# Row maxima of an 8192 x 8192 matrix: another order of the rows over the DMA engines, and one store per block

## The chip, the cores and the metric

The kernel runs on one core of a Trainium2 chip. The metric is the device time of one launch in microseconds: the median of three runs was 626.82 us (626.64 to 627.1). One more execution was taken with the hardware profiler; all readings of the trace are from that one.

## The reference

The input is a matrix of 8192 rows and 8192 columns in float32 (32 KB a row, 268.4 MB in all). The output has, for each row, the largest absolute value in it:

```python
def reference(x):
    return np.linalg.norm(x, ord=np.inf, axis=1)
```

## The kernel before

Each of the 128 partitions of the on-chip memory gets 64 of the rows. A tile `t` holds two rows of each partition (`B` = 2, `W` = 16384 columns, 64 KB a partition, 8.39 MB in all), and three such buffers rotate (`BUFS` = 3). All loads are issued by SyncE (SP) on one DMA queue, in the order of the program. Each waits until the buffer it writes is free, and in the tail for the semaphore that it takes over from an earlier DMA: eight completion semaphores go round over all the DMAs.

**Bulk.** 24 tiles (6 x `G`, `G` = 4) are loaded whole, one DMA each, L303. VectorE reduces each in one instruction (`absmax`, L296) to two columns of `r_bulk` (128 x 48). In memory a partition has eight rows in succession (256 KB) in each of the six blocks, and a tile takes two of them:

```python
x_b = x[:split].rearrange("(a p n b) c -> a n p (b c)", p=P, a=A, n=G, b=B)
```

**Tail.** The last 16 rows of each partition are 16 rows in succession (512 KB a partition). The first seven tail tiles are loaded in two to five pieces whose widths are listed in `TAIL` (L315), and every piece is reduced by itself to a column of `part`. The eighth is loaded in twelve pieces (`LAST`, L341), from 2176 columns down to 768. One instruction brings `part` together into 14 columns of `r_tail`; the last two columns of `r_tail` come from the last two pieces, each reduced together with the partial maxima of its row.

**Stores.** After the reduction of the tenth of the twelve pieces, ScalarE (ACT) stores `r_bulk` (L357). After the last reduction, SP stores `r_tail` (L359). These are all the DMAs there are besides the loads.

Functions run on the finished program (`start_first_load_early`, `drop_implied_waits`, `clear_partials_early`, `finish_on_pool`, `open_without_vector`): they put the first load ahead of the opening, drop waits that others imply, and let GpSimd end the program when the last store has landed. Neither these nor the reductions are touched by the change.

[...]

Of the kernel before, what the change touches and what calls it, by code (L numbers as in the profile page):

```python
# [12 lines left out]
F32 = mybir.dt.float32  # L13
# [4 lines left out]
TAIL = [  # L18
    [12672, 3712],
    [4992, 11392],  # L20
    [7040, 9344],
    [9344, 7040],
    [3584, 6784, 6016],
    [3968, 4224, 4736, 3456],
    [4096, 3584, 3200, 2944, 2560],
]
# [7 lines left out]


HEAD, STEP = 32, 8


def segments(loads, cols):

    out, at = [], 0
    for i, w in enumerate(loads):
        end = at + w
        while at < end:
            r = at // cols
            to = min(end, (r + 1) * cols)
            out.append((i, r, at - r * cols, to - at))
            at = to
    return out
# [201 lines left out]
@with_exitstack  # L251
def kernel(
    ctx: ExitStack,
    tc: tile.TileContext,
    x: bass.AP,
    out: bass.AP,
    G: int = 4,
    B: int = 2,
    BUFS: int = 3,
    PAD: int = 256,  # L260
    LINE: int = 128,
):
    nc = tc.nc
    P = nc.NUM_PARTITIONS
    rows, cols = x.shape
    W = B * cols


    n_tail = B * (len(TAIL) + 1)
    n_bulk_rows = rows // P - n_tail  # L270
    assert n_bulk_rows % (G * B) == 0
    A = n_bulk_rows // (G * B)
    split = n_bulk_rows * P
    x_b = x[:split].rearrange("(a p n b) c -> a n p (b c)", p=P, a=A, n=G, b=B)
    out_b = out[:split].rearrange("(a p n b) -> p a (n b)", p=P, a=A, n=G, b=B)
    x_t = x[split:].rearrange("(p t b) c -> t p (b c)", p=P, b=B)
    out_t = out[split:].rearrange("(p t) -> p t", p=P)

    outp = ctx.enter_context(tc.tile_pool(name="outp", bufs=1))
    sbuf = ctx.enter_context(tc.tile_pool(name="sbuf", bufs=BUFS))  # L280

    segs = [segments(loads, cols) for loads in TAIL]
    k_max = max(sum(r == b for _, r, _, _ in s) for s in segs for b in range(B))
    parts_of = [sum(r == b for r, _ in LAST) - 1 for b in range(B)]
    assert sum(parts_of) <= PAD

    r_bulk = outp.tile([P, A, G * B], F32)
    r_tail = outp.tile([P, n_tail], F32)
    part = outp.tile([P, n_tail - B, k_max], F32)
    used = [HEAD, A * G * B, n_tail, (n_tail - B) * k_max]  # L290
    gap = -sum(-(-n // STEP) * STEP for n in used) % LINE
    outp.tile([P, gap], F32, name="gap")
    nc.gpsimd.memset(part[:], 0.0)  # L293

    def absmax(o, i):
        return nc.vector.reduce_max(  # L296
            out=o, in_=i, axis=X, apply_absolute_value=True
        )

    for a in range(A):  # L300
        for n in range(G):
            t = sbuf.tile([P, W + PAD], F32, tag="t")
            nc.sync.dma_start(out=t[:, :W], in_=x_b[a, n])  # L303
            absmax(
                r_bulk[:, a, n * B : (n + 1) * B],
                t[:, :W].rearrange("p (b c) -> p b c", b=B),
            )

    for i, loads in enumerate(TAIL):
        t = sbuf.tile([P, W + PAD], F32, tag="t")  # L310
        todo = segs[i]
        seen = [0] * B
        at = 0
        for j, w in enumerate(loads):
            nc.sync.dma_start(out=t[:, at : at + w], in_=x_t[i][:, at : at + w])  # L315
            at += w
            for _, b, c, n in [s for s in todo if s[0] == j]:
                k, lo = seen[b], b * cols + c
                absmax(part[:, i * B + b, k : k + 1], t[:, lo : lo + n])
                seen[b] += 1  # L320

    def after(ins, first, kind):
        info = mybir.DependencyInfo(kind, mybir.DependencyReason.SCHED_ONLY)
        tc.add_manual_dep(ins.ins, first.ins.name, info, reason="order")


    t = sbuf.tile([P, W + PAD], F32, tag="t")
    left = parts_of[:]
    col = [0] * B
    at, slot = 0, {}  # L330
    ends = [w for _, w in LAST[-B:]]
    lo = W - sum(ends)
    for b in range(B):
        slot[b] = -(-lo // LINE) * LINE + ends[b]
        lo = slot[b] + parts_of[b]
    assert lo <= W + PAD
    for j, (b, w) in enumerate(LAST):
        final = left[b] == 0
        to = slot[b] - w if final else at
        frm = b * cols + col[b]  # L340
        nc.sync.dma_start(out=t[:, to : to + w], in_=x_t[len(TAIL)][:, frm : frm + w])  # L341
        col[b] += w
        if final:
            r = n_tail - B + b
            absmax(r_tail[:, r : r + 1], t[:, to : slot[b] + parts_of[b]])
        else:
            left[b] -= 1
            k = slot[b] + left[b]
            done = absmax(t[:, k : k + 1], t[:, to : to + w])
            at += w  # L350
        if j == 0:

            ins = absmax(r_tail[:, : n_tail - B], part[:])
            after(ins, done, mybir.DependencyClass.NoSync)
        if j == len(LAST) - 3:

            ins = nc.scalar.dma_start(out=out_b, in_=r_bulk[:])  # L357
            after(ins, done, mybir.DependencyClass.Sync)
    nc.sync.dma_start(out=out_t, in_=r_tail[:])  # L359
    nc.at_finalize(clear_partials_early)  # L360
    nc.at_finalize(drop_implied_waits)
    nc.at_finalize(start_first_load_early)
    nc.at_finalize(finish_on_pool)
    nc.at_finalize(open_without_vector)
# [30 lines left out]
```

## Time and profile before

| what | value |
|---|---|
| median of three runs | 626.82 us |
| the profiled execution, whole | 626.52 us |
| its span, first to last instruction | 623.9 us |
| VectorE busy | 552.4 us, 63 instructions |
| load queue (q1), share of 16 DMA engines' span | 99.7% |
| bytes read | 268.44 MB, 430 GB/s over the span |
| 24 bulk reductions | 413.3 us, 17.22 us each |

The profiler gives the start and duration of every instruction and every DMA packet, and for each wait what ended it. "SPq" and "ACTq" are the issuing sides of SP and ACT: an issue takes about 0.3 to 0.4 us there and the transfer goes on by itself. A packet record has a queue, a size, a start and a duration, but not the number of its DMA engine. In the chain of work, each step leads back from the last instruction to what released it. Groups are given by line, engine, operation and tiles, written as out<-in.

### The profile page before, as it was taken

To read this page: it belongs to the slowest core of one execution; us is meant where nothing else is said; L and a number is where in the kernel's file an instruction comes from. 1 tells how busy PE (TensorE), PEld (TensorE's weight loads), DVE (VectorE), ACT (ScalarE), POOL (GpSimd) and SP (SyncE) were. 2 spreads that over 40 slices of the span, in tenths; PEclk is the share of its full clock that TensorE was granted. 3 is DMA by queue.
4 is the path that set the end of the run, shared out by engine and by line. 5 is a ranking of instruction groups with operands and counts; after the bars stand their busy time and mean duration, and the time that the engine had idled before them with its cause. 6 is when DMAs were issued, how large, how long until landed. Compare 5 with 4: busy or idle time off the path is not lost.

```text
span 623.9 us, 151 instructions
## 1 busy us (share of the span) xinstructions
DVE 552.4 (89%) x63; POOL 0.3 (0%) x5
## 2 busy tenths in 40 slices
DVE  0588988889988899888898888988889999999999
POOL 0000000000000000000000000000000000000000
DMA  9999999999999999999999999999999999999998
GB/s 403 462 412 454 420 433 441 403 471 403 471 403 454 420 454 420 441 433 403 471 403 471 403 466 408 454 420 450 424 434 406 435 445 422 431 441 428 423 427 349
DMA packets 8849, 268.47 MB, mean 430 GB/s; under 512 B 1680, under 2 KB 1680, under 8 KB 3088
## 3 DMA queue, kind: packets, MB, share of 16 engines
q1 hardware_dynamic: 8064, 268.44, 99.7%
q10 hardware_dynamic: 784, 0.02, 0.1%
q14 instruction: 1, 0.01, 0.0%
HBM read 268.44 MB, written 0.03 MB: 430 GB/s over the span
## 4 chain that ended last, share of the span: by engine, by line
DMA 63%; DVE 36%; another core or an unknown queue 0%; DVEq 0%; issue 0%
DMA t<-in_x_dram 63%; DVE r_bulk L296 25%; DVE part L296 8%; DVE t L296 3%; DVEq L390 0%; DVE r_tail L296 0%
## 5 line engine op out<-in xcount | busy, mean ns | idle before, releaser
L296 DVE TENSOR_REDUCE r_bulk<-t 128x2 f32<-128x16384 f32 x24 | 413.3, 17220 | 70.5 <-DMA t<-in_x_dram 70.5
L296 DVE TENSOR_REDUCE part<-t 128x1 f32<-128x8192 f32 (+19 forms) x26 | 121.3, 4738 | 0.3
L296 DVE TENSOR_REDUCE t<-t 128x1 f32<-128x1792 f32 (+7 forms) x10 | 16.3, 1689 | 0.0
L296 DVE TENSOR_REDUCE r_tail<-t 128x1 f32<-128x772 f32 (+1 forms) x2 | 1.8, 947 | 0.0
L296 DVE TENSOR_REDUCE r_tail<-part 128x14 f32<-128x42 f32 x1 | 0.2, 185 | 0.0
L293 POOL MEMSET part<- 128x42 f32 x1 | 0.1, 133 | 0.0
L379 POOL MEMSET const-bfloat16-1.0<- 128x1 bf16 x1 | 0.1, 102 | 0.0
L379 POOL MEMSET const-uint8-127<- 128x1 uint8 x1 | 0.1, 102 | 0.0
L379 POOL MEMSET const-float32-0.0<- 128x1 f32 x1 | 0.1, 99 | 0.2 <-issue 0.2
L379 POOL MEMSET const-float32-1.0<- 128x1 f32 x1 | 0.1, 99 | 0.0
## 6 DMA issues: line engine op xcount, KB each, us to landing
t<-in_x_dram SPq DMA_DIRECT2D x2, 4672.0 KB, 37.5
t<-in_x_dram SPq DMA_DIRECT2D x2, 3520.0 KB, 36.2
t<-in_x_dram SPq DMA_DIRECT2D x1, 6336.0 KB, 36.4
t<-in_x_dram SPq DMA_DIRECT2D x1, 5696.0 KB, 40.5
t<-in_x_dram SPq DMA_DIRECT2D x2, 1792.0 KB, 34.3
t<-in_x_dram SPq DMA_DIRECT2D x1, 3392.0 KB, 37.6
t<-in_x_dram SPq DMA_DIRECT2D x1, 3008.0 KB, 44.2
t<-in_x_dram SPq DMA_DIRECT2D x1, 2496.0 KB, 27.3
```

The source lines that it names most:

```text
L293: nc.gpsimd.memset(part[:], 0.0)
L296: return nc.vector.reduce_max(out=o, in_=i, axis=X, apply_absolute_value=True)
L379: nc = _bacc.Bacc("TRN2", target_bir_lowering=False, num_devices=1)
```

## The change

The rows are dealt out otherwise. The 32 tiles, bulk and tail alike, are taken from four blocks of 11, 13, 5 and 3 tiles (`BLOCKS`). Within a block of n tiles, E is n x 64 KB, the n pairs of rows that one partition reads in succession. Partition 8e + i reads its rows at (16 i + e) x E from the block's start: e, from 0 to 15, is the outer dimension of the source of a load, i, from 0 to 7, the next. By the words of the change, e is the DMA engine and i the row of that engine. The first two blocks (24 tiles) are the bulk, the other two (8 tiles) the tail.

As a partition's rows of a block lie together, each block has its own store: `r_bulk` goes out in two stores and the first ten columns of `r_tail` in a third, all issued by ACT behind the same reduction as the one store before; the last six columns of `r_tail` go out from SP at the end, as all 16 did before. The sizes of all tiles, loads and reductions stay, and the order of the loads too. `r_bulk` loses a dimension without a change of size.

```diff
+LANES = 16
+BLOCKS = (11, 13, 5, 3)
+BULK = 2
...
-    x_b = x[:split].rearrange("(a p n b) c -> a n p (b c)", p=P, a=A, n=G, b=B)
-    out_b = out[:split].rearrange("(a p n b) -> p a (n b)", p=P, a=A, n=G, b=B)
-    x_t = x[split:].rearrange("(p t b) c -> t p (b c)", p=P, b=B)
-    out_t = out[split:].rearrange("(p t) -> p t", p=P)
+    tiles, outs, at = [], [], 0
+    for n in BLOCKS:
+        span = slice(at, at + n * B * P)
+        at = span.stop
+        v = x[span].rearrange("(i e n b) c -> n e i (b c)", e=LANES, n=n, b=B)
+        tiles += [v[k] for k in range(n)]
+        outs.append(out[span].rearrange("(i e m) -> e i m", e=LANES, m=n * B))
+    n_bulk = n_bulk_rows // B
+    x_t = tiles[n_bulk:]
...
-            nc.sync.dma_start(out=t[:, :W], in_=x_b[a, n])
+        nc.sync.dma_start(out=t[:, :W], in_=tiles[n])
...
-            nc.sync.dma_start(out=t[:, at : at + w], in_=x_t[i][:, at : at + w])
+            nc.sync.dma_start(
+                out=t[:, at : at + w], in_=x_t[i][:, :, at : at + w]
+            )
...
+    def store(engine, blocks, r, order):
+        first = min(b for b in range(len(BLOCKS)) if (b < BULK) == (blocks[0] < BULK))
+        for b in blocks:
+            lo = B * sum(BLOCKS[first:b])
+            ins = engine.dma_start(
+                out=outs[b], in_=r[:, lo : lo + B * BLOCKS[b]]
+            )
+            if order is not None:
+                after(ins, order, mybir.DependencyClass.Sync)
...
-        nc.sync.dma_start(out=t[:, to : to + w], in_=x_t[len(TAIL)][:, frm : frm + w])
+        nc.sync.dma_start(
+            out=t[:, to : to + w], in_=x_t[len(TAIL)][:, :, frm : frm + w]
+        )
...
-            ins = nc.scalar.dma_start(out=out_b, in_=r_bulk[:])
-            after(ins, done, mybir.DependencyClass.Sync)
-    nc.sync.dma_start(out=out_t, in_=r_tail[:])
+            store(nc.scalar, range(BULK), r_bulk, done)
+            store(nc.scalar, range(BULK, len(BLOCKS) - 1), r_tail, done)
+    store(nc.sync, [len(BLOCKS) - 1], r_tail, None)
```

More of the change, by code (lines that the diff above doesn't have):

```diff
@@ L256 @@
     out: bass.AP,
-    G: int = 4,
     B: int = 2,
@@ L270 @@
     n_bulk_rows = rows // P - n_tail
-    assert n_bulk_rows % (G * B) == 0
-    A = n_bulk_rows // (G * B)
-    split = n_bulk_rows * P
-    x_b = x[:split].rearrange("(a p n b) c -> a n p (b c)", p=P, a=A, n=G, b=B)
-    out_b = out[:split].rearrange("(a p n b) -> p a (n b)", p=P, a=A, n=G, b=B)
-    x_t = x[split:].rearrange("(p t b) c -> t p (b c)", p=P, b=B)
-    out_t = out[split:].rearrange("(p t) -> p t", p=P)
+    assert sum(BLOCKS) * B * P == rows
+    tiles, outs, at = [], [], 0
[7 more added lines that the diff above has]
+    x_t = tiles[n_bulk:]
     outp = ctx.enter_context(tc.tile_pool(name="outp", bufs=1))
@@ L285 @@
     assert sum(parts_of) <= PAD
-    r_bulk = outp.tile([P, A, G * B], F32)
+    r_bulk = outp.tile([P, n_bulk_rows], F32)
     r_tail = outp.tile([P, n_tail], F32)
     part = outp.tile([P, n_tail - B, k_max], F32)
-    used = [HEAD, A * G * B, n_tail, (n_tail - B) * k_max]
+    used = [HEAD, n_bulk_rows, n_tail, (n_tail - B) * k_max]
     gap = -sum(-(-n // STEP) * STEP for n in used) % LINE
@@ L298, in absmax @@
         )
-    for a in range(A):
-        for n in range(G):
-            t = sbuf.tile([P, W + PAD], F32, tag="t")
-            nc.sync.dma_start(out=t[:, :W], in_=x_b[a, n])
[L304 to L307, printed above, removed]
+    for n in range(n_bulk):
+        t = sbuf.tile([P, W + PAD], F32, tag="t")
+        nc.sync.dma_start(out=t[:, :W], in_=tiles[n])
+        absmax(
+            r_bulk[:, n * B : (n + 1) * B],
+            t[:, :W].rearrange("p (b c) -> p b c", b=B),
+        )
     for i, loads in enumerate(TAIL):
@@ L340 @@
         frm = b * cols + col[b]
-        nc.sync.dma_start(out=t[:, to : to + w], in_=x_t[len(TAIL)][:, frm : frm + w])
+        nc.sync.dma_start(
+            out=t[:, to : to + w], in_=x_t[len(TAIL)][:, :, frm : frm + w]
+        )
         col[b] += w
```

## Prediction

> **What bounds the kernel now.** I read the page first: the span, the busy time of each engine, the DMA queues.
>
> ```profile
> span 623.9 us, 151 instructions
> DVE 552.4 (89%) x63; POOL 0.3 (0%) x5
> ...
> q1 hardware_dynamic: 8064, 268.44, 99.7%
> ...
> HBM read 268.44 MB, written 0.03 MB: 430 GB/s over the span
> ...
> L296 DVE TENSOR_REDUCE r_bulk<-t 128x2 f32<-128x16384 f32 x24 | 413.3, 17220 | 70.5 <-DMA t<-in_x_dram 70.5
> ```
>
> Two engines work: the DMA engines, which bring the 268.44 MB, and VectorE, which takes maxima. The load queue q1 fills 99.7% of the 16 DMA engines' span, so about 2 us of 623.9 are not transfer. VectorE is idle 70.5 us ahead of the 24 bulk reductions, always for a load. The bound is the transfer, and only two things can shorten it: faster packets, or a shorter start and end.
>
> Next the chain of work that ended last, in order of time, for the bulk's period:
>
> ```profile
> 118.71 17.23 DVE r_bulk L296
> 135.94 0.02 issue
> 135.95 40.75 DMA t<-in_x_dram
> 176.71 0.02 issue
> 176.73 17.23 DVE r_bulk L296
> ```
>
> From 118.71 to 176.73, three tiles pass in 58.02 us: 19.34 us for 8.39 MB, 433.8 GB/s, or 27.1 GB/s for each engine. The step 17.23 + 40.75 says that a freed buffer is at once loaded again: two more loads are always queued, so the DMA engines have no hole between tiles.
>
> Is there slack in that rate? The trace's packet records answer. A 64 KB packet lasts 2.418 us in the median, the shortest of all 3,072 too; the smaller packets of the tail lie on one line with it (3,072 B 0.121 us, 50,688 B 1.872 us: 8 ns and 27.2 GB/s). After 280 us no bulk packet is over 2.418 us by more than 4 ns, and no size in the tail has one above its own median. The only slow packets to speak of are the first one of each engine: 2.54 to 3.36 us, mean 2.92. They start from 0.99 to 2.05 us and end from 3.85 to 4.79 us.
>
> The third view is the timeline of the end, with the stores' times to landing from the list of DMA issues.
>
> ```profile
> 621.32 1.81 DVE L296 TENSOR_REDUCE r_tail<-t 128x1 f32<-128x772 f32 x2
> 621.43 0.41 ACTq L357 DMA_DIRECT2D out_dram<-r_bulk  x1
> 623.15 0.35 SPq L359 DMA_DIRECT2D out_dram<-r_tail  x1
> ```
>
> ```profile
> out_dram<-r_bulk ACTq DMA_DIRECT2D x1, 24.0 KB, 2.5
> out_dram<-r_tail SPq DMA_DIRECT2D x1, 8.0 KB, 1.4
> ```
>
> The last load has its 16 increments from 621.36 to 622.01 us; its reduction follows (0.95 us), then the last store at 623.15, which lands 1.4 us later, at 624.56. The store from ACT has landed at 623.96, before that. This execution took 626.52 us for a span of 623.9, 0.30 below the median of the runs, 626.82. I sum against 626.52 and carry the difference over to the median.
>
> **The new row order, in the bulk and the tail.** Bytes, tiles, packet sizes, reductions, buffers and the order of the loads stay: 24 bulk tiles of one 64 KB piece per partition, then the same widths in the tail. What moves is the address: today the rows of neighbouring partitions lie 256 KB apart in the bulk and 512 KB in the tail, so eight partitions on are 2 and 4 MB; after, sixteen pieces E x 64 KB apart, with odd E. In the steady state this removes nothing, as there is nothing above 2.418 us to remove. All excess over 2.418 us in the bulk is 11.8 engine-us: 8.0 in the first 16 packets, 3.8 in the other 3,056. Over 16 engines that is 0.50 and 0.24 us. If the first packets are slow because the 16 engines start at addresses a power of two apart, the 0.50 go. The upper bound takes the late starts with it: all 16 start by 1.17 us (as ten of them do) and last 2.418, and the last ends at 3.59 instead of 4.79, 1.20 us earlier, and with the 0.24 it is 1.44. The lower bound is nothing: a first packet can be slow for being first. I take 0.50: the slow packets are the ones that run together in the first 3 us, and the late starters, which ran with less company, were shorter (2.67 and 2.54). The cost side of the new order has no row; it is a rival below.
>
> [...]
>
> **The shape of the loads.** The source gets a dimension more (16 x 8 rows). SP's issue of a load takes 0.328 us, the very first 0.367; ACT's issue, the one DMA with two counted dimensions (6 x 128), takes 0.406. So a load's issue may grow by 0.04 to 0.08 us. Only the first is on the path, and I take 0.04; all others are issued with two or more loads queued, 19 us of cover in the bulk. In the last tile a load is issued when the load eight places before it has landed, with some 10 us of transfers queued or more; without that cover 0.08 x 12 would be 1 us.
>
> **The stores.** One ACT store of 768 records of 32 B becomes three, of 128 pieces each (88, 104 and 40 B). They wait for the same reduction (the end of the load of 896 columns, 621.40), so they are issued from 621.43 at about 0.45 us each: 621.43, 621.88, 622.33. From the row of today's: first packet 0.95 us after issue, 0.83 us from the last packet to landing, and 8 pieces per engine instead of 48. The third lands near 622.33 + 0.95 + 0.1 + 0.83 = 624.2, ahead of 624.56: cost nothing, cover 0.35 us. Nothing else is queued on ACT but the closing drain, now done at 622.03, then near 622.95, still ahead of SP's last issue. All three start after the last load's packets have ended (621.75), so they take no transfer time. Two more completion semaphores are taken. Today's store has the semaphore after the last two loads', so the loads keep theirs. Were the stores ahead, those two loads would wait for loads that land by 616.4 us, with 3,840 columns (4.5 us) still queued: no hole. VectorE's last two reductions write other columns of `r_tail` than the third store reads; the loads into `t` show today that different columns of a tile don't wait for each other.
>
> The last store, on SP and on the path, gets pieces of 24 B instead of 64. Rows: 64 B land 0.36 us after their last packet, 32 B 0.83. So it costs 0 to 0.47 us, and I take 0.20, since today's 32 B store had six times the records.
>
> **Sum.** -0.50 + 0.04 + 0.20 = -0.26 us: 626.26 for the execution profiled, 626.56 on the median; forecast 626.5. Its own range is from -1.44 (625.4) to +0.08 + 0.47 (627.4). 0.2% is 1.25 us, about what a measurement of this kernel can tell from no change.
>
> **Rivals.** *A clean start, faster.* The whole 1.44 us goes and the last store costs nothing: 625.4, just beyond 0.2% (625.57). For it: the first packets' starts spread 1.06 us, and 0.65 us of spread is still there in the last load's increments, so what is lost at the start is never made up. Against: it needs every term at its end.
>
> *New distances, new collisions, slower.* Today the engines keep one set of distances over the whole bulk, and the excess dies out by 280 us: they seem to have fallen into step. After, the distances change at four block starts, and E was set by arithmetic, not by a row of this trace. Price: a round of collisions as at the start is 0.50 to 0.74 us. One at each of three further block starts gives 626.5 + 3 x 0.74 = 628.7; one at each of 32 tiles 626.5 + 16 = 642.5. It decides from three further rounds on. Against: the reduction's step shows the bulk at its ceiling with 2 MB distances, so collisions seem cheap once engines are apart.
>
> *Another split over the engines, slower.* Today every load raises its semaphore 16 times, one for each engine, from a source counted 128. If the 16 x 8 source were spread over eight engines, 619 us of packets become 1,238 and the time about 1,245; any smaller loss of side-by-side work lies between. For it: no load of this shape is in the trace. Against: the outer count is 16.
>
> [...]
>
> *A wait for the store.* If the last two reductions waited for the third ACT store (landing near 624.2 instead of starting at 621.3), it would cost some 2.9 us: 629.4.
>
> *The engines' rows are not the ones said.* Then the spacing is another, the first packets stay as they are, and the stores' 0.24 alone counts: 627.1. It lies in the forecast's own range.
>
> **Chances.** Forecast with its neighbours within 0.2%: 0.62. Clean start 0.12. Collisions 0.14, half of them at most 628.7. Another split 0.08. The wait 0.04. So faster 0.12, same 0.62, slower 0.26. The range runs from 625.3 to 628.8 and leaves out the split, the wait and half of the collisions, 0.19.
>
> **What would show it.** Right: first packets near 2.42 us and the second reduction of the bulk before 41.35; the bulk's step still 19.34 us a tile; three ACT stores landed before SP's; the last one 1.4 to 1.9 us to landing. Wrong: a step above 19.4 us, in one block or all (collisions; twice that, the split); idle time of VectorE for a store at the end; or a first landing no earlier than 22.05, which would mean that the start doesn't depend on addresses.

## Result: 1,286 us, twice the time of before

The changed kernel took 1286.17 us in the median of four runs (1278.53 to 1291.13), against 626.78 of the kernel before, also four runs: a ratio of 2.0508, 95% interval 2.0405 to 2.0611. The forecast was 626.5 with a range to 628.8.

The page of the changed kernel, with the rows that were read of before:

```profile
span 1284.6 us, 153 instructions
...
DVE 555.1 (43%) x63; POOL 0.3 (0%) x5
...
q1 hardware_dynamic: 8064, 268.44, 100.0%
...
HBM read 268.44 MB, written 0.03 MB: 209 GB/s over the span
...
L303 DVE TENSOR_REDUCE r_bulk<-t 128x2 f32<-128x16384 f32 x24 | 413.3, 17220 | 576.6 <-DMA t<-in_x_dram 576.6
```

The same 8,064 load packets carry the same bytes, and VectorE's bulk reductions last the same 17.22 us. The queue's share is 100%: the 16 DMA engines are not idle, they are busy all the time and move half as much in the same time. VectorE's wait for loads ahead of the bulk reductions grows from 70.5 to 576.6 us.

The chain of work, for one step of the bulk (start, duration, what):

```profile
124.57 17.22 DVE r_bulk L303
141.79 23.14 another core or an unknown queue
164.93 0.02 issue
164.95 17.22 DVE r_bulk L303
```

One tile passes in 164.95 - 124.57 = 40.38 us, where it was 19.34. The chain can't name what ended the 23.14 us; the group row above can: the load. The last bulk reduction starts at 972.7 instead of 466.5 us, 506.2 later, and from there to the end it is 311.9 instead of 157.4 us, 154.5 more. Together that is the whole growth of the span, 660.7 us. The loss runs through bulk and tail: a step of the bulk takes 2.09 times as long, the stretch from the last bulk reduction to the end 1.98 times.

In the packet records a 64 KB packet lasts 5.105 us in the median (5% to 95%: 4.89 to 5.13) instead of 2.418, and each load still raises its semaphore 16 times. So all 16 engines work, each 64 KB packet takes 2.11 times as long, and the first of each engine does already (mean 5.02). The smaller packets of the tail lose less, down to 1.58 times for 3,072 B (0.191 instead of 0.121 us).

The records show a rhythm, too. Taken sixteen at a time in order of start, one packet for each engine, and without the first four rounds, the 64 KB packets of every fourth round last 4.91 us in the mean and those of the three rounds between 5.11. In the kernel before, there is no such rhythm (2.418 to 2.421).

The issue and the landing of the stores, and the end of the timeline:

```profile
out_dram<-r_bulk ACTq DMA_DIRECT2D x1, 11.0 KB, 1.9
out_dram<-r_bulk ACTq DMA_DIRECT2D x1, 13.0 KB, 2.3
out_dram<-r_tail ACTq DMA_DIRECT2D x1, 5.0 KB, 1.9
out_dram<-r_tail SPq DMA_DIRECT2D x1, 3.0 KB, 1.9
```

```profile
1281.31 0.96 DVE L303 TENSOR_REDUCE r_tail<-t 128x1 f32<-128x772 f32 x1 [0.42 <-DMA t<-in_x_dram]
1282.21 0.61 ACTq L338 DMA_DIRECT2D out_dram<-r_tail  x1
1282.42 0.96 DVE L303 TENSOR_REDUCE r_tail<-t 128x1 f32<-128x774 f32 x1 [0.16 <-DMA t<-in_x_dram]
1283.41 0.59 SPq L338 DMA_DIRECT2D out_dram<-r_tail  x1
```

VectorE waits for no store, and the last one takes 1.9 us to landing instead of 1.4, so the stores add some 0.5 us to the end. What has to be explained is the packet.

### The profile page after: what moved, and what is told of

Read it like the earlier page. It is cut to its first block, busy times and chain, and to the rows that moved or that the text cites. A ratio compares the mean times of both kernels' runs of the same rounds, so it can differ in the third digit from the quotient of the medians.

```text
span 1284.6 us, 153 instructions
## 1 busy us (share of the span) xinstructions
DVE 555.1 (43%) x63; POOL 0.3 (0%) x5
## 3 DMA queue, kind: packets, MB, share of 16 engines
q1 hardware_dynamic: 8064, 268.44, 100.0%
## 4 chain that ended last, share of the span: by engine, by line
another core or an unknown queue 54%; DVE 38%; DMA 8%; SPq 0%; issue 0%; DVEq 0%
DVE r_bulk L303 32%; DMA t<-in_x_dram 8%; DVE part L303 5%; SPq L321 0%; SPq L359 0%; DVE r_tail L303 0%; DVEq L303 0%
## 5 line engine op out<-in xcount | busy, mean ns | idle before, releaser
L303 DVE TENSOR_REDUCE r_bulk<-t 128x2 f32<-128x16384 f32 x24 | 413.3, 17220 | 576.6 <-DMA t<-in_x_dram 576.6
```

The lines of the kernel that those rows point to most:

```text
L303: return nc.vector.reduce_max(out=o, in_=i, axis=X, apply_absolute_value=True)
```

## The experiments

Three theories stood at first. Except for the second, each kernel below was timed once; the main effects are of a factor of two. A: the 16 x 8 source hands each DMA engine eight neighbouring partitions, and engines then meet on the write side, in the on-chip memory. B: the new distances collide on the read side, in the main memory. C: a load of this shape is slow in itself, wherever it reads and writes. Addresses and shape came together in the change, so the first two runs take them apart.

**Shape without the odd distances.** The changed kernel with

```diff
-BLOCKS = (11, 13, 5, 3)
-BULK = 2
+BLOCKS = (8, 8, 8, 4, 4)
+BULK = 3
```

> The changed kernel with its 16 x 8 source, but blocks of 8, 8, 8, 4 and 4 tiles, so that all distances are powers of two times 64 KB again. Theory A (the split: the 16 x 8 source hands each DMA engine eight neighbouring partitions, and engines then meet at the write side) and theory C (a load of this shape is slow by itself, wherever it reads and lands): nothing changes, 64 KB packets near 5.1 us, about 1,286 us. Theory B (the odd distances collide in the main memory): packets back at 2.42 us, about 627 to 628 us.

Measured: 1292.6 us, 64 KB packets 5.121 us in the median. The powers of two don't bring the rate back; odd distances are not needed for the loss.

**Odd distances without the shape.** The changed kernel with a source counted 128, all else kept, the four stores too:

```diff
-        v = x[span].rearrange("(i e n b) c -> n e i (b c)", e=LANES, n=n, b=B)
+        v = x[span].rearrange("(p n b) c -> n p (b c)", n=n, b=B)
...
-        outs.append(out[span].rearrange("(i e m) -> e i m", e=LANES, m=n * B))
+        outs.append(out[span].rearrange("(p m) -> p m", m=n * B))
```

> The changed kernel with its blocks of 11, 13, 5 and 3 tiles, its four stores and its odd distances, but a source counted 128: partition p reads at p x E. A and C: packets at 2.42 us, 626 to 627 us; if the slow first packets of before come from distances that are powers of two, their mean falls from 2.92 towards 2.42 us and the time by about 0.5 us. The three ACT stores and the 24 B pieces of the last one should cost 0 to 0.5 us (0.2 in the prediction). B: packets well over 2.42 us, up to 5.1, and a time up to 1,286 us.

Measured: 626.56 us (11 runs), ratio to before 0.9997, interval 0.9988 to 1.0006: no difference. Its page and its chain:

```profile
span 624.2 us, 153 instructions
...
q1 hardware_dynamic: 8064, 268.44, 99.7%
...
HBM read 268.44 MB, written 0.03 MB: 430 GB/s over the span
```

```profile
118.54 17.23 DVE r_bulk L303
135.77 0.02 issue
135.79 41.17 DMA t<-in_x_dram
176.96 0.02 issue
176.98 17.23 DVE r_bulk L303
```

Three tiles in 58.44 us here (57.96 in the next step), 2.418 us a packet: the loss is gone with the shape. B falls for these distances, though not for every order of reading: partition p reads at p x E here, and not partition 8e + i at (16 i + e) x E. And in both runs that were slow the shape may also have changed where each engine writes, so A and C still stand together.

**The same loads to another place.** A smaller kernel loads 64 tiles of 64 partitions with a source counted 16 x 4 and the E of the change, without the finishing functions. It reduces only the first 1,024 columns of each row, in two halves of 32 partitions; only the first partition differs between two runs. By A the two may differ, if engines meet in one place and not in the other; no run before these shows which places those are.

```diff
-LO = 0
+LO = 32
...
             t = sbuf.tile([128, W], F32, tag="t")
             nc.sync.dma_start(out=t[LO : LO + Q, :], in_=v[j])
```

> 64 tiles of 64 partitions (0 to 63), source counted 16 x 4 with E = 11, 13, 5, 3 (twice), the same bytes and 64 KB packets in all; it reduces only the first 1024 columns of each row, so that VectorE is never the bound. [...]

> The same kernel with the tiles on partitions 32 to 95: the same source, addresses, shape, engines and packets, only the place in the on-chip memory differs. [...] B and C: no difference from the run on partitions 0 to 63, near 5.1 us and 1,290 us.

Measured: 1323.45 us on partitions 0 to 63, 632.66 us on 32 to 95; packets of 5.125 and 2.418 us. The pages, first on 0 to 63, then on 32 to 95:

```profile
span 1321.7 us, 314 instructions
...
HBM read 268.44 MB, written 0.03 MB: 203 GB/s over the span
...
L44 DVE TENSOR_REDUCE r<-t 32x2 f32<-32x2048 f32 x128 | 291.2, 2275 | 1027.9 <-DMA t<-in_x_dram 1027.1
```

```profile
span 630.9 us, 314 instructions
...
HBM read 268.44 MB, written 0.03 MB: 426 GB/s over the span
...
L44 DVE TENSOR_REDUCE r<-t 32x2 f32<-32x2048 f32 x128 | 291.4, 2276 | 336.9 <-DMA t<-in_x_dram 336.1
```

Same source, shape and packets, and VectorE is busy the same 291 us; only its wait for loads differs, 1027 against 336 us. B and C both fall, B for the order (16 i + e) x E as well: the place in the on-chip memory decides. Partitions 0 to 31 are not slow in themselves, as the kernel before fills them at 2.418 us a packet. What sets partitions 0 to 63 apart from 32 to 95 no run shows; measured are 203 against 426 GB/s.

**Is the 16 x i form needed at all?** The same two places with a uniform source counted 64.

```diff
-SHAPED = True
+SHAPED = False
...
         if SHAPED:
             v = x[span].rearrange("(i e n b) c -> n e i (b c)", e=16, n=n, b=B)
             o = out[span].rearrange("(i e m) -> e i m", e=16, m=n * B)
         else:
             v = x[span].rearrange("(p n b) c -> n p (b c)", n=n, b=B)
             o = out[span].rearrange("(p m) -> p m", m=n * B)
```

> As the run of 64 tiles on partitions 0 to 63, but with a source counted 64 at a uniform distance of E, as the kernel before has it with 128 (again only the first 1024 columns of each row are reduced). A (the write side decides): 4.9 to 5.1 us a packet, 1,300 to 1,325 us, as with the source counted 16 x 4. Rival (the 16 x i form of the source is needed for the loss): 2.42 us and about 632 us.

> The same uniform source counted 64 on partitions 32 to 95 (only the first 1024 columns of each row are reduced). Both: 2.42 us a packet and about 632 us; an outcome near 5.1 us would say that engines do not have neighbouring partitions when the source is uniform.

Measured: 1319.24 us with 5.118 us a packet on 0 to 63, 632.5 us with 2.418 on 32 to 95. The form is not needed on 64 partitions: a uniform source is as slow where the place is bad.

**Pairs, or all traffic together?** All 16 engines work in the runs on the two places, so they don't say whether two engines that meet are enough or only the sum of all traffic is too much. Two more kernels load only four tiles of 128 partitions, with fewer engines (`K` = 2 and `K` = 4), and reduce the first 1,024 columns of each row:

```diff
-            v = x[span].rearrange("(i e n b) c -> n e i (b c)", e=16, n=n, b=B)
+    v = x[: n * B * P].rearrange("(i e n b) c -> n e i (b c)", e=K, n=n, b=B)
```

> Four loads of 128 partitions with a source counted 2 x 64, so that two DMA engines do the work; the other 28 tiles are left out, as are all but the first 1024 columns of each row in the reductions, so only packet times are read. [...]

> The same with a source counted 4 x 32: four engines walk 32 neighbouring partitions each. [...]

The queue's share of 16 engines' span says how many work, first with K = 2, then with K = 4; 2/16 is 12.5%, 4/16 is 25%. Which partitions each of them has, no record says:

```profile
q1 hardware_dynamic: 520, 33.55, 12.4%
```

```profile
q1 hardware_dynamic: 528, 33.55, 24.5%
```

Measured: with two engines 2.418 us a packet in the median, and all but one of the 512 under 2.5. With four, 5.06 us in the median of the first 32 packets, then less and less: by load the mean is 4.76, 4.30, 4.03 and 3.81 us, 4.22 in all. VectorE's timeline shows it, first of the run with four engines, then with two (start, duration, operation, idle before):

```profile
156.53 2.29 DVE L34 TENSOR_REDUCE r<-t 128x2 f32<-128x2048 f32 x1 [155.60 <-DMA t<-in_x_dram]
295.03 2.29 DVE L34 TENSOR_REDUCE r<-t 128x2 f32<-128x2048 f32 x1 [136.22 <-DMA t<-in_x_dram]
424.73 2.29 DVE L34 TENSOR_REDUCE r<-t 128x2 f32<-128x2048 f32 x1 [127.42 <-DMA t<-in_x_dram]
547.63 2.29 DVE L34 TENSOR_REDUCE r<-t 128x2 f32<-128x2048 f32 x1 [120.61 <-DMA t<-in_x_dram]
```

```profile
158.11 2.29 DVE L34 TENSOR_REDUCE r<-t 128x2 f32<-128x2048 f32 x1 [157.18 <-DMA t<-in_x_dram]
312.62 2.29 DVE L34 TENSOR_REDUCE r<-t 128x2 f32<-128x2048 f32 x1 [152.23 <-DMA t<-in_x_dram]
```

The first load lands at nearly the same time with four engines as with two: the two more brought next to nothing. The kernel moves 56 GB/s there, where four engines at 27.1 would be 108, by estimate; both are far below the 208 of the changed kernel's bulk, so no limit on the sum explains it. But the loss shrinks: some packets later last 2.42 us again (none in the first two loads, 12 and 25 of 128 in the last two).

The records show how. Each packet starts within 30 ns of where another ends, so they can be strung into four chains of 128 packets, one for each engine. In every chain the durations go by fours. In two chains the first packet of each four gets shorter, from 4.2 us to 2.7, and late in the run the second one too; in the other two it is the last one, from 5.1 us to 2.42, and then the third. That is what two engines would show that walk from place to place, four packets to a place, one of them more and more ahead: it reaches the next place alone, and the other ends alone at the place before. That the engines of a pair drift apart is read from this, as no record names an engine. In the changed kernel nothing of that growth is seen: each load's 64 KB packets have a median of 5.10 to 5.11 us, and none is under 4.55.

## Why the prediction was wrong

**The step that failed** is "What moves is the address". By what the runs leave over, the new source also moved the destination of each engine: which partitions it writes, and so which engines write to one place at one time. The prediction's sum had no cost for that; a 64 KB packet went from 2.418 to 5.105 us and a tile from 19.34 to 40.38. If two engines that meet share the 27.1 GB/s that one brings alone, a packet takes 2 x 2.418 = 4.84 us, by estimate; 5.1 was measured, and what the remaining 5% are is open. That the 16 x 8 source gives an engine eight neighbours, and that engines meet by twos, is concluded, not seen, as no packet record names its engine; which partitions make up one place, no run shows. The rhythm of four fits it: a load gives an engine eight packets, so two fours, as if the engine changed its place at every fourth packet, where the 4.91 us are; on partitions 0 to 63, where a load gives an engine only four packets, the rhythm is no more than 0.05 us. The run with the shape alone (5.121 us), the two places (5.125 against 2.418) and two against four engines (2.418 against 5.06 at first) fit it too. The 128-count source keeps the full rate (2.418 us) and has no rhythm of four (2.418 to 2.421), so by the same reading it isn't dealt out in eight neighbours walked in step; how it is dealt out, no run shows.

**The rival that came true** was "another split over the engines", and it had 0.08. Its price, 1,245 us, was near by luck, for its mechanism was not the one that acted: it counted engines, and all 16 work. Its counterargument, "the outer count is 16", answers how many engines take part and not where each writes. That engines could meet where they write had no chance of its own.

**The start** (-0.50) didn't come. With odd distances and the old split the first 16 packets lasted 3.06 us in the mean against 2.92 before, and the others had 0.55 us of excess per engine against 0.24. VectorE's first reduction began at 21.93 us instead of 22.05, a quarter of the 0.50 (one profile of each). So these slow first packets don't need distances that are powers of two. The clean start (0.12) goes with it.

**The loads' issue** (0.04 to 0.08) was mis-sized: the 16 x 8 source takes SP 0.536 us instead of 0.328, the first one 0.646 instead of 0.367, and the first packet starts at 1.42 instead of 0.99 us. ACT's two-dimension store (0.406) was a bad neighbour. It is hidden for all loads but the first, as the queue's 100% shows.

**The stores** were right for the ACT part: in the run with the old split the third lands at 624.30 us (624.2 was worked out) and the last at 624.86. The 24 B pieces of the last store cost nothing there: 1.4 us to landing as before. In the changed kernel, with the 16 x 8 form, it is 1.9, the upper end of what the prediction allowed.

**Collisions from new distances** (0.14) and **the wait for a store** (0.04) didn't happen: 0.9997 in the one case, and 2.418 us a packet on partitions 32 to 95 for the order (16 i + e) x E; VectorE idle only for loads in the other.

No version here beats the kernel before; the odd distances alone equal it within 0.12%.

## What to carry to other kernels

A load has two sides. A source regrouped with the same bytes and the same packets may also move where each engine writes, and here the place of the same load made 203 or 426 GB/s. So before regrouping a source, ask what it does to the destination, and time the same load into another place. Full DMA share with half the GB/s is the sign to look for: here the queue was at 100.0% with 209 GB/s, and at 99.7% with 430 before, so packet durations (5.105 instead of 2.418 us) showed the loss where busy shares didn't. Before the change, every bulk packet lasted nearly the same and the queue was at 99.7%; other addresses alone won nothing then (ratio 0.9997), so the question was what else the change moved.

## What was not expected of the hardware

The same load runs at 203 GB/s into partitions 0 to 63 and at 426 GB/s into 32 to 95. Four engines brought the first load in about as late as two did (at 156.5 us, with two at 158.1), as if two that meet brought together what one brings alone. With four engines part of the rate comes back (4.76 to 3.81 us a packet over four loads), as if each pair drifted out of step; with 16 engines, over 24 loads of the bulk, it did not (5.10 to 5.11 us in the median of each load).
